# Side b of a two-sided attention layer: its queries three units ahead, its maxima two units ahead

## The chip, the cores and the metric

The kernel runs on one core of a Trainium2 chip. The metric is the device time of one execution in microseconds (us). TensorE (PE in the profile) multiplies matrices; its weight loads are listed as PEld. VectorE (DVE), ScalarE (ACT) and GpSimd (POOL) work on tiles, and SyncE (SP) issues every DMA of this kernel. Each engine takes its instructions from a queue of its own, in order.

## The reference

A decoder layer on 1024 tokens of width 1024, batch 1. After a modulated layer norm one wide projection gives the inputs of two attention branches and their gates:

```
qa = _rope(q_a...)                                    # side a: 2 groups of 4 heads, width 64
o_cmp, p_cmp = _compressed_attention(qa, kc, vc)      # over 63 compressed keys
sel_idx = _select_blocks(p_cmp, S)                    # 8 of 16 key blocks per query
o_sel = _selected_attention(qa, k_s, v_s, sel_idx)
o_win = _banded_attention(qa, k_w, v_w, 512)
qb = _rope(q_b...)                                    # side b: 2 groups of 4 heads
o_b = _banded_attention(qb, k_b, v_b, 128, sinks[l])  # softmax with one sink logit per head
merged = sigmoid(gm_a) * (y_a @ w_up_a) + sigmoid(gm_b) * (y_b @ w_up_b)
out = merged @ w_out;  x = layer_norm(ALPHA*x + gate*out) * ln_g + ln_b
```

Every score is divided by 8 (the square root of the head width) ahead of its softmax. All is float32; the kernel reaches it with pairs of narrower matmuls (a high part and the rest).

## The kernel before

**Stages.** First the layer norm, the modulation and the key and value projections; then one long attention stage (`Att.run`); then the outputs' transposes, the up projections, the output projection and the last norm.

**Units.** `Att.run` walks over 32 units (side, group, tile of 128 queries): (a,0,0) to (a,1,7), then (b,0,0) to (b,1,7). A unit has three parts.
- `C(u)` makes its queries. ACT copies q into the high half of `qat` (L752) and POOL takes the rest (L753); ACT copies q into `qbt` (L755); PE turns `qat` (L759) into a PSUM bank, and ACT copies that into `qa` (L761). On side a it also does the compressed attention and the block selection.
- `M(u)` finds each query's maximum. PE multiplies `qa` with the keys (`bank<-Ks,qa` and `bank<-Kw,qa` in the profile; side b has two banks of two matmuls per unit), DVE takes the masked maximum of each head (L878) and the negated result into `qbt` (L882); on side b POOL and ACT make the sink's term `esink` (L885, L886); PE turns `qbt` (L890) and ACT copies that into `qb` (L892). C and M share three PSUM banks, taken in turn.
- Per key tile, `score` multiplies the keys with `qa` and with `qb` into one bank, so that the maximum is already taken off. DVE adds a mask where one is needed (L907), ACT takes the exponential `e` (L909 or L911) and its f16 copy `ph` (L914), POOL the rest `pl` (L917); `weigh` then multiplies `pl` and `ph` with the values. A side b unit has two key tiles (one for tile 0). `combine` scales the result and SP stores it (`o_raw<-q`, L958).

**Order.** While unit i is weighed, M of unit i+1 and C of unit i+2 are made (`part` after each key tile, `finish` at the end). There are two `qbt` tiles and three `qa` tiles. Between these steps `feed` puts in "fill": projections that the attention does not need yet, in blocks (`gm_block`, four weight loads and 48 matmuls of 512 columns; side b's query projections; side b's keys). A fill weight comes by a DMA into one of three `raw` tiles (issued by SP at L245 or L257), ACT casts its high part into `whl` (L248, L259), POOL subtracts for the low part (L249, L260), and PE uses both with `uH` and `uL`. There are ten `whl` tiles. A scheduler then sets the order on each engine from its own model of time; what it made is fixed in the program.

The 1/8 is folded into the query's rotation tables: three ACT multiplications (L1173) make `qcos` and `qsin` from `cos`, `nsin` and `sin`. POOL copies or adds `sink` as it comes from memory (L1147).

Of the kernel before, what the change touches and what calls it, by code (L numbers as in the profile page):

```python
# [7 lines left out]
F32 = mybir.dt.float32  # L8
# [19 lines left out]
POFF = math.log(16.0)  # L28
XB = 8
# [686 lines left out]
class Att:  # L716


    def __init__(self, L, q, work):

        self.L, self.q, self.w = L, q, work
        self.ms, self.st, self.av = Banks(L, MS), Banks(L, ST), Banks(L, (5,))
        nc = L.nc
        self.nc = nc
        self.U = {}
        self.qbt = []
        for i in range(2):
            q = work.tile([128, 4, 128], F32R, name=f"qbt{i}")
            nc.gpsimd.tensor_copy(q.rearrange("p h d -> p (h d)"), L.mk[:, 128:129].to_broadcast([128, 512]))
            self.qbt.append(q)  # L730
        self.p0 = work.tile([128, 128], F32, name="p0")[:, :68]
        nc.gpsimd.memset(self.p0, 0.0)
        self.n, self.last = 0, []
        self.off = [True, True]
# [9 lines left out]
    def C(self, u):  # L744
# [6 lines left out]
        qbt = st["qbt"] = self.qbt[self.n % 2]  # L751
# [8 lines left out]
        qa = st["qa"] = w.tile([128, 512], F32R, name="qa", tag="qa", bufs=3)  # L760
        nc.scalar.copy(qa, tr.bitcast(F32).rearrange("p h t -> p (h t)"))  # L761
        yield 0.25
        if side == "b":
            self.rows_off(self.n % 2)
            return
# [4 lines left out]
        t = w.tile([128, 4, 64], F32, name="cs", tag="cs")  # L770
        nc.vector.tensor_tensor(t, sc[:, :, 1, :], L.vis[:, qt, None, :].to_broadcast([128, 4, 64]), op=OP.add)
        nc.vector.tensor_tensor(t, t, sc[:, :, 0, :], op=OP.add)
        sm = w.tile([128, 4, 8], F32, name="csm", tag="csm", bufs=2)[:, :, :4]
# [3 lines left out]
        nc.scalar.activation(e, t, AF.Exp)  # L777
# [4 lines left out]
        pc = w.tile([128, 4, 64], F32, name="cp", tag="cp")  # L782
# [6 lines left out]
        if qt >= 4:  # L789
            nc.vector.tensor_reduce(self.p0[:, 1:64], pc[:, :, 0:63].rearrange("p h c -> p c h"), axis=AX.X, op=OP.add)  # L790
            im = w.tile([128, 4, 16], F32, name="imp", tag="imp")
# [3 lines left out]
            m8 = w.tile([128, 40], F32, name="m8", tag="m8")[:, :8]  # L795
            nc.vector.max(m8, im[:, 1])
            nc.vector.match_replace(im[:, 2], m8, im[:, 1], -3e38)
            sel = st["sel"] = w.tile([128, 16], F32, name="sel", tag="sel", bufs=3)
# [9 lines left out]
        pT = w.tile([128, 2, 128], F32, name="pT", tag="pT")  # L808
# [20 lines left out]
    def M(self, u):  # L829
# [53 lines left out]
        if side == "b":  # L883
            es = st["es"] = w.tile([128, 2, 4], F32, name="esink", tag="esink", bufs=3)
            nc.gpsimd.tensor_tensor(es[:, 0], L.sink[:, g * 4:g * 4 + 4], qbt.bitcast(F32)[:, :, 80 + g], op=OP.add)  # L885
            nc.scalar.activation(es[:, 1], es[:, 0], AF.Exp, bias=L.poff)  # L886
# [9 lines left out]
    def score(self, u, br, kt):  # L896
# [9 lines left out]
        if kt == qt or edge:  # L906
            nc.vector.tensor_tensor(e.rearrange("p (h q) -> p h q", h=4), ps.rearrange("p (h q) -> p h q", h=4),  # L907
                                    L.mkt[:, int(edge), None, :].to_broadcast([128, 4, 128]), op=OP.add)
            nc.scalar.activation(e, e, AF.Exp, bias=L.poff)  # L909
        else:  # L910
            nc.scalar.activation(e, ps, AF.Exp, bias=L.poff)  # L911
# [48 lines left out]
    def run(self, units, fill, ratio, values):  # L960
# [52 lines left out]

        def part(f, u, k, n):
# [4 lines left out]
            while s[1] < want:  # L1019
                s[1] += 1  # L1020
                try:
                    feed(next(s[0]))
                except StopIteration:
                    s[1] = 1 << 30

# [15 lines left out]
        for gi, grp in enumerate(groups):  # L1041
# [24 lines left out]
            if k == n:  # L1066
                if ui + 1 < len(units):
                    finish(self.M, units[ui + 1])
                if ui + 2 < len(units):
# [54 lines left out]
def run_layer(L):  # L1124
# [22 lines left out]
    nc.sync.dma_start(L.sink, bass.AP(tensor=I["sinks"].tensor, offset=I["sinks"].offset, ap=[[0, 128], [1, 8]]))  # L1147
    acc = L.acc1
# [45 lines left out]
    def q_chunk(side, g, rows):  # L1194
# [3 lines left out]
        for t in ORD[side][g]:  # L1198
# [5 lines left out]
            L.rope(q, a[:, :256], t, qp, nc.vector, L.qcos, L.qsin)  # L1204
# [96 lines left out]
    for cm in (wk_cm, kvb[0], k0_cm, k1_cm, qp_cm):  # L1301
        L.close(cm)
# [214 lines left out]
```

## Time and profile before

| | |
|---|---|
| median of 3 runs | 943.93 us (943.79 to 946.45) |
| the profiled execution: its time, its span | 945.29 us, 943.5 us |
| PE busy, PEld busy | 914.3 us (97%), 787.0 us (83%) |
| POOL, DVE, ACT busy | 575.6, 550.2, 471.4 us |
| mean granted TensorE clock | 0.994 of full speed |

The span is the time from the first instruction to the last in the profile; the time around it holds 1.8 us more. The profiled execution was 1.4 us over the median. A busy engine is one that has an instruction under way; for PE this counts pipelined matmuls, so that small gaps between two matmuls do not show. Times in the trace are counted from the span's start.

### The profile page before, as it was taken

The numbers are of one execution on the slowest core, as the hardware profiler recorded it, in microseconds if no ns is written. First come the engines' busy times: TensorE is split into PE (matmuls) and PEld (weight loads), VectorE is DVE, ScalarE is ACT, GpSimd is POOL, SyncE is SP. The second block draws the span as 40 slices with busy tenths as digits, with TensorE's granted clock in tenths as the row PEclk, the third lists the DMA queues.
The fourth block names the chain that finished last, engine by engine and source line by source line (L and its number), as shares of the span: only waits on it lengthen the run. The fifth ranks groups of instructions, "written<-read, shape, count | busy, mean of one in ns | idle before, by whom it ended". The sixth has DMA issues, their size and how long they took to land.

```text
span 943.5 us, 18610 instructions
## 1 busy us (share of the span) xinstructions
PE 914.3 (97%) x6592; PEld 787.0 (83%) x6592; DVE 550.2 (58%) x1621; ACT 471.4 (50%) x984; POOL 575.6 (61%) x808
## 2 busy tenths in 40 slices
PE   7899998999999999999999999999899999999996
PEld 5689997788899888898899888789788888888885
DVE  7843356554776554465786643456552666454687
ACT  5846344344555566646555555756663664532100
POOL 7867565365768766767677766756753245535822
PEclk9999999999999999999999999999989999999999
DMA  9913232212202211202201212030222977655312
GB/s 329 293 29 115 81 91 57 79 51 79 68 7 53 62 57 57 63 13 70 76 7 35 74 58 75 22 101 13 69 62 75 371 249 221 192 188 193 130 69 110
DMA packets 93278, 95.40 MB, mean 101 GB/s; under 512 B 7616, under 2 KB 72192, under 8 KB 93184
## 3 DMA queue, kind: packets, MB, share of 16 engines
q1 hardware_dynamic: 93184, 94.21, 31.9%
q8 instruction: 52, 0.85, 0.4%
q14 instruction: 42, 0.34, 0.1%
HBM read 73.21 MB, written 20.97 MB: 100 GB/s over the span
## 4 chain that ended last, share of the span: by engine, by line
PE 69%; DMA 8%; DVE 8%; POOL 7%; ACT 3%; issue 3%; SPq 1%; DVEq 0%; POOLq 0%; ACTq 0%
PE bank L108 65%; DMA sg<-gm_raw 2%; POOL z L1421 2%; DMA raw<-in_w_ada_dram 2%; DMA raw<-in_w_out_dram 1%; DMA raw<-in_w_in_dram 1%; POOL rstd L1444 1%; DVE res L1450 1%; POOL pl L917 1%; PE bank L890 1%; DVE jk L878 1%; DMA x<-in_x_dram 1%; PE bank L759 1%; POOL whl L260 1%; PE bank L1327 1%
## 5 line engine op out<-in xcount | busy, mean ns | idle before, releaser
L108 PE MATMUL bank<-whl,uH 128*128 128x256 f32 (+3 forms) x1168 | 270.6, 322 | 4.6 <-ACT uH L449 4.3
L108 PE MATMUL bank<-uH,whl 128*128 128x512 f32 x768 | 247.5, 397 | 0.0
L917 POOL TENSOR_TENSOR pl<-e,ph 128x512 f16<-128x512 f32 x162 | 188.1, 1167 | 66.4 <-ACT ph L914 58.1
L108 PEld LDWEIGHTS bank<-whl,uH 128*128 128x128 f32 x1168 | 197.9, 189 | 22.2 <-ACT uH L449 5.3
L108 PE MATMUL bank<-whl,uL 128*128 128x256 f32 (+3 forms) x584 | 181.3, 319 | 0.0
L108 PEld LDWEIGHTS bank<-uH,whl 128*128 128x128 f32 x768 | 142.1, 189 | 26.8
L260 POOL TENSOR_TENSOR whl<-raw,whl 128x256 fp32r<-128x256 f32 x128 | 99.1, 779 | 86.6 <-ACT whl L259 78.6
L108 PE MATMUL bank<-uL,whl 128*128 128x512 f32 x384 | 151.3, 394 | 0.0
L108 PEld LDWEIGHTS bank<-whl,uL 128*128 128x128 f32 x584 | 110.1, 189 | 7.4
L914 ACT CAST ph<-e 128x512 f16<-128x512 f32 x162 | 98.4, 618 | 25.1 <-PE bank L108 23.1
L878 DVE CUSTOM_DVE_ANT_0 jk<-bank,mk 128x256 bf16<-128x256 f32 (+3 forms) x168 | 73.9, 440 | 30.0 <-PE bank L108 25.4
L911 ACT ACTIVATE e<-bank,poff 128x512 f32<-128x512 f32 x92 | 62.0, 687 | 54.0 <-PE bank L108 50.3
L108 PEld LDWEIGHTS bank<-uL,whl 128*128 128x128 f32 x384 | 72.6, 189 | 14.9
L259 ACT CAST whl<-raw 128x256 fp32r<-128x256 f32 x128 | 50.8, 404 | 66.0 <-PE bank L108 42.2
L108 PE MATMUL bank<-yH,whl 128*128 128x512 f32 x256 | 79.1, 393 | 0.0
L108 PEld LDWEIGHTS <-pl 128*128 128x128 f16 x648 | 59.4, 98 | 17.1 <-issue 11.2
L249 POOL TENSOR_TENSOR whl<-raw,whl 128x256 fp32r<-128x256 f32 (+3 forms) x60 | 53.3, 895 | 24.1 <-ACT whl L248 22.8
L907 DVE TENSOR_TENSOR e<-bank,mkt 128x512 f32<-128x512 f32 x70 | 47.5, 688 | 33.0 <-PE bank L108 27.9
L108 PEld LDWEIGHTS <-ph 128*128 128x128 f16 x1296 | 65.2, 97 | 0.8 <-issue 0.5
L909 ACT ACTIVATE e<-e,poff 128x512 f32<-128x512 f32 x70 | 49.8, 721 | 30.5 <-DVE e L907 30.2
L248 ACT CAST whl<-raw 128x256 fp32r<-128x256 f32 (+3 forms) x72 | 34.2, 480 | 60.9 <-DMA raw<-in_w_out_dram 36.8
L108 PEld LDWEIGHTS bank<-yH,whl 128*128 128x128 f32 x256 | 47.7, 188 | 10.1 <-issue 0.5
(292 smaller groups left out, 1730.0 us busy)
## 6 DMA issues: line engine op xcount, KB each, us to landing
raw<-in_w_in_dram SPq DMA_DIRECT2D x136, 128.0 KB, 2.2
gm_raw<-gmo SPq DMA_DIRECT2D x48, 256.0 KB, 2.0
wada<-in_w_ada_dram SPq DMA_DIRECT2D x16, 512.0 KB, 6.0
sg<-gm_raw SPq DMA_DIRECT2D x32, 256.0 KB, 3.2
x<-in_x_dram SPq DMA_DIRECT2D x8, 512.0 KB, 5.1
o_raw<-q SPq DMA_DIRECT2D x32, 128.0 KB, 1.9
o<-o_raw SPq DMA_DIRECT2D x8, 512.0 KB, 6.7
z<-gm_raw SPq DMA_DIRECT2D x16, 256.0 KB, 6.7
```

Source lines behind the costliest of these rows:

```text
L108: return self.nc.tensor.matmul(out, l, r, start=start, stop=stop, skip_group_check=True)
L248: self.cast = nc.scalar.copy(h, raw).ins
L249: low = eng.tensor_tensor(l, raw, h.bitcast(F32), op=OP.subtract).ins
L259: nc.scalar.copy(hl[:, 0], raw)
L260: eng.tensor_tensor(hl[:, 1], raw, hl.bitcast(F32)[:, 0], op=OP.subtract)
L878: nc.vector.tensor_tensor_reduce(o, src, m, 1.0, -3e38, OP.add, OP.max, mx[:, h, g if side == "b" else bi, slots[h]:slots[h] + 1])
L907: nc.vector.tensor_tensor(e.rearrange("p (h q) -> p h q", h=4), ps.rearrange("p (h q) -> p h q", h=4), L.mkt[:, int(edge), None, :].to_bro ...
L909: nc.scalar.activation(e, e, AF.Exp, bias=L.poff)
L911: nc.scalar.activation(e, ps, AF.Exp, bias=L.poff)
L914: nc.scalar.copy(ph, e)
L917: eng.tensor_tensor(pl, e, ph, op=OP.subtract)
L1421: nc.gpsimd.tensor_scalar(z[:, t, :], z[:, t, :], ALPHA, None, op0=OP.mult)
```

## The change

It has three parts, and the scheduler orders the whole anew.

1. For side b the three parts are taken further ahead. While unit i of side b is weighed, the new `jobs` asks for `finish(M, i+1)` (the last turn of `qbt`) and all of `C(i+3)` after the first key tile, and for the scores and maxima of `M(i+2)` (`all_but` stops ahead of the turn) after the last.
2. For that, side b gets a third `qbt` tile and a fourth `qa` tile. They lie in a pool that takes the place of side a's own tiles (the compressed attention's), which move into a pool of their own that is closed when side b's first C is made. POOL fills the new `qbt` once.
3. The 1/8 moves from the query's tables into the exponentials (`scale=SCALE`), so the three multiplications at L1173 go; `sink` is multiplied by 8 once on POOL.

```diff
+SCALE = 0.125
+EORD = (1,0,1)
...
+        self.wx, self.wx_cm = L.pool("sidea", 1, side="right")
...
-        qbt = st["qbt"] = self.qbt[self.n % 2]
+        if side == "a":
+            qbt = self.qbt[self.n % 2]
+        else:
+            if len(self.qbt) == 2:
+
+                L.close(self.wx_cm)
+                self.wx, self.wx_cm = L.pool("sideb", 1, side="right")
+                self.qbt.append(self.wx.tile([128, 4, 128], F32R, name="qbt2"))
+                nc.gpsimd.tensor_copy(self.qbt[2].rearrange("p h d -> p (h d)"), L.mk[:, 128:129].to_broadcast([128, 512]))
+                self.nb = 0
+            i = (1, 2, 0)[self.nb % 3]
+            if i < 2:
+                self.rows_off(i)
+            qbt = self.qbt[i]
+            st["n"] = self.nb
+            self.nb += 1
+        st["qbt"] = qbt
...
-        qa = st["qa"] = w.tile([128, 512], F32R, name="qa", tag="qa", bufs=3)
+        if side == "b" and st["n"] % 4 == 1:
+            qa = self.wx.tile([128, 512], F32R, name="qa3", tag="qa3")
+        else:
+            qa = w.tile([128, 512], F32R, name="qa", tag="qa", bufs=3)
...
-            nc.scalar.activation(es[:, 1], es[:, 0], AF.Exp, bias=L.poff)
+            nc.scalar.activation(es[:, 1], es[:, 0], AF.Exp, bias=L.poff, scale=SCALE)
...
-            nc.scalar.activation(e, ps, AF.Exp, bias=L.poff)
+            nc.scalar.activation(e, ps, AF.Exp, bias=L.poff, scale=SCALE)
...
+        def all_but(f, u):
+
+            s = get(f, u)
+            while s[1] < 3:
+                s[1] += 1
+                feed(next(s[0]))
...
+        def jobs(ui):
+
+            b = 2 * NT
+            if ui == b - 2:
+                return [(finish, self.C, b + 1, 0)]
+            if ui == b - 1:
+                return [(finish, self.M, b, -6), (finish, self.C, b + 2, -3), (all_but, self.M, b + 1, -1)]
+            if ui >= b:
+                e = EORD
+                return [(finish, self.M, ui + 1, e[0]), (all_but, self.M, ui + 2, e[1]), (finish, self.C, ui + 3, e[2])]
+            return []
...
-            if ui + 1 < len(units):
+            if ui < 2 * NT - 1:
                 part(self.M, units[ui + 1], k, n)
-            if ui + 2 < len(units):
                 part(self.C, units[ui + 2], k, n)
+            for f, g, x, w in jobs(ui):
+                if x < len(units) and k == (w if w > 0 else n + w):
+                    f(g, units[x])
...
+    nc.gpsimd.tensor_scalar(L.sink, L.sink, 1.0 / SCALE, None, op0=OP.mult)
...
-    L.qcos = qp.tile([128, 8, 32], F32, name="qcos")
-    qsin = qp.tile([128, 2, 8, 32], F32, name="qsin")
-    L.qsin = (qsin[:, 0], qsin[:, 1])
-    for o, x in ((L.qcos, L.cos), (L.qsin[0], L.nsin), (L.qsin[1], L.sin)):
-        nc.scalar.mul(o, x, 0.125)
```

Apart from the operations of part 3, every engine keeps its order up to the weighing of (a,1,6), where the first C of side b is made (at 567 us in the trace of before). From there on the order is new. Three places of it follow; line numbers of the changed kernel are larger (L759 is L778 there, L890 is L912, L108 is L110, L257 is L259, L958 is L980, L259 is L261, L761 is L784, L892 is L914, L909 is L931, L914 is L936).

**PE, around the queries of (b,1,4).** Before: the turn of `qat` of (b,1,4), the first matmuls of two scores, the maxima's scores of (b,1,4), the turn of `qbt` of (b,1,3), the turn of `qat` of (b,1,5).

```order
L108 MATMUL bank_10386<-uL,whl 128x512
L759 MATMUL bank_10472<-idr,qat 128x128 x4
L108 MATMUL bank_10459<-qa,Kw_934 128x512
L108 MATMUL bank_10502<-qa,Kw_934 128x512
L108 MATMUL bank_10518<-Kw_934,qa 128x256 x2
L890 MATMUL bank_10452<-idr,qbt_1882 128x128 x4
L759 MATMUL bank_10583<-idr,qat 128x128 x4
```

With the change, from the turn of `qat` of (b,1,4) to its maxima's first scores (the row of bank_10538; the row of bank_10417 is the second half of those of (b,1,3)):

```order
L778 MATMUL bank_10359<-idr,qat 128x128 x4
L110 MATMUL bank_10391<-qb,Kw_930 128x512
L110 MATMUL bank_10417<-Kw_930,qa 128x256 x2
L110 MATMUL bank_10462<-qb,Kw_930 128x512
L110 MATMUL bank_10538<-Kw_930,qa 128x256 x2
```

and a little further on, from the second half of the maxima's scores of (b,1,5) to the turn of its `qbt` (L912), with the turn of `qat` of (b,1,6) (L778) and its maxima's first scores (bank_10716):

```order
L110 MATMUL bank_10634<-Kw_930,qa_10497 128x256 x2
L110 MATMUL bank_10662<-qa,Kw_930 128x512
L110 MATMUL bank_10662<-qb,Kw_930 128x512
L778 MATMUL bank_10594<-idr,qat 128x128 x4
L110 MATMUL bank_11316<-uH,whl 128x512
L912 MATMUL bank_10672<-idr,qbt_8325 128x128 x4
L110 MATMUL bank_10716<-Kw_930,qa 128x256 x2
```

The turn of the next unit's `qat` no longer stands right behind these; the distance from a turn to the scores that use it grew from two matmuls to four at (b,1,4), and is two short pieces at (b,1,6).

**SP, the fill weights between the stores of side b.** Before: one load (the first of a block of four), the stores of (b,0,4) to (b,0,7), one load, the store of (b,1,0), two loads, the store of (b,1,1), five loads.

```order
L257 DMA raw_10938<-in_w_in_dram 128x2x128
L958 DMA o_raw_73<-q_7573 128x256
L958 DMA o_raw_73<-q_7661 128x256
L958 DMA o_raw_73<-q_7739 128x256
L958 DMA o_raw_73<-q_7823 128x256
L257 DMA raw_10943<-in_w_in_dram 128x2x128
L958 DMA o_raw_73<-q_9701 128x256
L257 DMA raw_10948<-in_w_in_dram 128x2x128
L257 DMA raw_10953<-in_w_in_dram 128x2x128
L958 DMA o_raw_73<-q_9798 128x256
L257 DMA raw_11152<-in_w_in_dram 128x2x128
L257 DMA raw_11157<-in_w_in_dram 128x2x128
```

With the change, the same block of four (now raw_10944 to raw_10959) and the first load of the next block stand ahead of the stores of (b,0,5) to (b,1,0); behind these come three loads, the store of (b,1,1), and raw_11296.

```order
L259 DMA raw_10954<-in_w_in_dram 128x2x128
L1306 DMA gm_raw_72<-gmo_9780 128x512
L259 DMA raw_10959<-in_w_in_dram 128x2x128
L259 DMA raw_11158<-in_w_in_dram 128x2x128
L980 DMA o_raw_73<-q_7660 128x256
L980 DMA o_raw_73<-q_7738 128x256
L980 DMA o_raw_73<-q_7822 128x256
L980 DMA o_raw_73<-q_9848 128x256
L259 DMA raw_11163<-in_w_in_dram 128x2x128
L259 DMA raw_11168<-in_w_in_dram 128x2x128
L980 DMA o_raw_73<-q_9947 128x256
L259 DMA raw_11296<-in_w_in_dram 128x2x128
```

Four loads moved from behind those stores to ahead of them. (Between the last two loads and the last store stands raw_11173, of the same form.)

**ACT, the casts ahead of the queries' copies.** Before, ahead of the copy `qa` of (b,1,4), which is qa_10477:

```order
L892 CAST qb_10313<-bank3_10308 128x512
L755 CAST qbt1_1884<-q_10078 128x4x64
L259 CAST whl_10950<-raw_10948 128x256
L259 CAST whl_10955<-raw_10953 128x256
L259 CAST whl_11154<-raw_11152 128x256
L259 CAST whl_11159<-raw_11157 128x256
L909 ACTIVATE e_10321<-e_10321,poff_124 128x512
L761 CAST qa_10477<-bank2_10472 128x512
```

With the change, ahead of the copies `qb` of (b,1,4), which is qb_10588, and `qa` of (b,1,6), which is qa_10599:

```order
L261 CAST whl_11170<-raw_11168 128x256
L261 CAST whl_11175<-raw_11173 128x256
L931 ACTIVATE e_10528<-e_10528,poff_124 128x512
L914 CAST qb_10588<-bank3_10583 128x512
L936 CAST ph_10531<-e_10528 128x512
L261 CAST whl_11298<-raw_11296 128x256
L774 CAST qbt1_1880<-q_10518 128x4x64
L931 ACTIVATE e_10576<-e_10576,poff_124 128x512
L784 CAST qa_10599<-bank4_10594 128x512
```

Four casts stood in a row ahead of a query's copy; now there are two and one, with other work between.

## Rows read from the trace of the kernel before

**Rows 1.** Busy time by stage: stretch (us), its length, then per engine busy us and count of instructions, the mean granted clock, the share of DMA, GB/s.

```profile
575.00:615.00 40.00, 39.30 (x356) 31.31 (x354) 15.36 (x54) 30.36 (x62) 29.37 (x41) 1.00 0.14 44
615.00:665.00 50.00, 48.51 (x468) 44.12 (x467) 29.73 (x114) 30.50 (x66) 31.04 (x54) 1.00 0.17 54
665.00:725.00 60.00, 56.98 (x452) 48.07 (x452) 27.96 (x100) 32.33 (x68) 33.83 (x51) 0.94 0.22 60
725.00:943.50 218.50, 210.37 (x979) 174.81 (x977) 136.87 (x201) 70.82 (x133) 95.94 (x75) 0.99 0.57 191
```

**Rows 2.** The same view in pieces of one us, in the third of these stretches.

```profile
680.00:681.00 1.00, 0.38 (x1) 0.06 (x1) 0.76 (x5) 0.63 (x2) 0.15 (x1) 1.00 0.63 141
681.00:682.00 1.00, 0.08 (x1) 0.08 (x1) 0.00 (x0) 1.00 (x3) 0.58 (x1) 1.00 0.47 125
...
683.00:684.00 1.00, 0.31 (x3) 0.34 (x3) 0.50 (x3) 1.00 (x3) 0.94 (x4) 0.66 0.29 86
684.00:685.00 1.00, 1.00 (x6) 0.90 (x5) 0.00 (x0) 1.00 (x4) 1.00 (x2) 0.50 0.00 0
...
690.00:691.00 1.00, 1.00 (x16) 0.73 (x15) 0.00 (x0) 0.00 (x0) 0.00 (x0) 0.92 0.19 74
```

**Rows 3.** PE in order of time there: start, us, engine, line, operation and tiles, forms, count, and in brackets the idle time ahead of it and what ended it.

```profile
676.26 0.62 PE L108 MATMUL bank<-uH,whl 128*128 128x512 f32 x2
676.72 0.40 PE L108 MATMUL bank<-uL,whl 128*128 128x512 f32 x1
...
679.02 0.46 PE L759 MATMUL bank<-idr,qat 128*128 128x128 f32 x4
...
681.92 0.50 PE L108 MATMUL bank<-Kw,qa 128*128 128x256 f32 x2 [1.55 <-ACT qa L761]
...
683.69 0.72 PE L759 MATMUL bank<-idr,qat 128*128 128x128 f32 x4 [0.97 <-DVE mx L878]
```

**Rows 4.** PE's other waits in side b, from the same view.

```profile
603.15 0.19 PE L108 MATMUL bank<-Vw,pl 128*128 128x65 f16 x1 [0.48 <-POOL pl L917]
...
637.38 0.54 PE L890 MATMUL bank<-idr,qbt 128*128 128x128 f32 x4 [0.27 <-DVE qbt L882]
...
638.75 0.20 PE L108 MATMUL bank<-Vs,pl 128*128 128x65 f16 x1 [0.53 <-POOL pl L917]
...
660.26 0.46 PE L759 MATMUL bank<-idr,qat 128*128 128x128 f32 x4
661.40 0.53 PE L890 MATMUL bank<-idr,qbt 128*128 128x128 f32 x4 [0.68 <-DVE qbt L882]
...
705.31 0.53 PE L890 MATMUL bank<-idr,qbt 128*128 128x128 f32 x4 [0.41 <-DVE qbt L882]
```

**Rows 5.** ACT in order of time ahead of the wait at 681.92.

```profile
676.87 0.79 ACT L259 CAST whl<-raw 128x256 fp32r<-128x256 f32 x2 [2.44 <-DMA raw<-in_w_in_dram]
...
680.37 0.40 ACT L259 CAST whl<-raw 128x256 fp32r<-128x256 f32 x1 [1.48 <-DMA raw<-in_w_in_dram]
680.68 0.72 ACT L909 ACTIVATE e<-e,poff 128x512 f32<-128x512 f32 x1
681.30 0.56 ACT L761 CAST qa<-bank 128x512 fp32r<-128x512 f32 x1
```

**Rows 6.** SP in order of time: the issues of DMAs; a row of several stands for the time from the first to the last.

```profile
643.72 23.52 SPq L958 DMA_DIRECT2D o_raw<-q  x4
670.98 0.38 SPq L257 DMA_DIRECT2D raw<-in_w_in_dram  x1
...
673.01 1.08 SPq L257 DMA_DIRECT2D raw<-in_w_in_dram  x2
...
675.84 6.14 SPq L257 DMA_DIRECT2D raw<-in_w_in_dram  x5
```

**Rows 7.** DVE in order of time: two maxima of one bank and the reduction into `qbt`.

```profile
680.19 0.42 DVE L878 CUSTOM_DVE_ANT_1 jk<-bank,mk 128x256 bf16<-128x256 f32 x1
...
680.66 0.18 DVE L882 TENSOR_REDUCE qbt<-mx 128x8 fp32r<-128x24 f32 x1
```

**Rows 8.** The page, part 6: the loads of the fill weights (count, KB each, median us from issue to landing).

```profile
raw<-in_w_in_dram SPq DMA_DIRECT2D x136, 128.0 KB, 2.2
```

**Rows 9.** The line of the copy after the turn of `qat`: count, duration in ns (least, median, most), first and last start.

```profile
L761 ACT CAST qa<-bank x32: 564/580/595, 146.4 to 705.2; 128x512 fp32r<-128x512 f32 x32
```

**Rows 10.** ACT by line and form: an exponential without a scale, and the multiplications that go, which are activations with a constant scale of 0.125.

```profile
L777 ACT ACTIVATE cs<-cs 128x256 f32<-128x256 f32 x16 | 6.6, 414 | 20.6 <-POOL cs L775 20.6
...
L1173 ACT ACTIVATE qcos<-cos 128x256 f32<-128x256 f32 x1 | 0.4, 413 | 0.0
```

**Rows 11.** The sink's load, POOL around 30 us, and POOL's fill of a `qbt` tile at the start of the stage.

```profile
L1147 SPq DMA_DIRECT2D sink<-in_sinks_dram x1: 3072/3072/3072, 23.2 to 23.2; - x1
...
DMA to landing us min/median/max: 6.3/6.3/6.3
...
24.73 0.22 POOL L536 TENSOR_SCALAR lnv<-lnv 128x1 f32<-128x1 f32 x1
...
28.93 1.25 POOL L249 TENSOR_TENSOR whl<-raw,whl 128x496 fp32r<-128x496 f32 x1 [0.73 <-ACT whl L248]
31.70 4.31 POOL L450 TENSOR_TENSOR uL<-lnT,uH 128x256 fp32r<-128x256 f32 x5 [1.53 <-ACT uH L449]
...
L729 POOL CAST qbt<-mk 128x512 fp32r<-128x512 f32 x2 | 1.2, 605 | 0.0
```

More of the change, by code (lines that the diff above doesn't have):

```diff
@@ L759, in C @@
             self.last.append(nc.tensor.transpose(tr[:, h, :], qat[:, h].rearrange("p a d -> p (a d)"), L.idr).ins)
-        qa = st["qa"] = w.tile([128, 512], F32R, name="qa", tag="qa", bufs=3)
+        if side == "b" and st["n"] % 4 == 1:
+            qa = self.wx.tile([128, 512], F32R, name="qa3", tag="qa3")
+        else:
+            qa = w.tile([128, 512], F32R, name="qa", tag="qa", bufs=3)
+        st["qa"] = qa
         nc.scalar.copy(qa, tr.bitcast(F32).rearrange("p h t -> p (h t)"))
@@ L763, in C @@
         if side == "b":
-            self.rows_off(self.n % 2)
             return
@@ L769, in C @@
                              L.kcd[:, g].rearrange("p i c -> p (i c)"), True, True).ins)
-        t = w.tile([128, 4, 64], F32, name="cs", tag="cs")
+        t = self.wx.tile([128, 4, 64], F32, name="cs", tag="cs")
         nc.vector.tensor_tensor(t, sc[:, :, 1, :], L.vis[:, qt, None, :].to_broadcast([128, 4, 64]), op=OP.add)
         nc.vector.tensor_tensor(t, t, sc[:, :, 0, :], op=OP.add)
-        sm = w.tile([128, 4, 8], F32, name="csm", tag="csm", bufs=2)[:, :, :4]
+        sm = self.wx.tile([128, 4, 8], F32, name="csm", tag="csm", bufs=2)[:, :, :4]
         nc.vector.tensor_reduce(sm[:, 0], t, axis=AX.X, op=OP.max)
@@ L776, in C @@
         e = t
-        nc.scalar.activation(e, t, AF.Exp)
+        nc.scalar.activation(e, t, AF.Exp, scale=SCALE)
         yield 0.45
@@ L781, in C @@
         nc.gpsimd.tensor_tensor(e, e, sm[:, 2, :, None].to_broadcast([128, 4, 64]), op=OP.mult)
-        pc = w.tile([128, 4, 64], F32, name="cp", tag="cp")
+        pc = self.wx.tile([128, 4, 64], F32, name="cp", tag="cp")
         nc.vector.scalar_tensor_tensor(pc.rearrange("p h c -> p (h c)"), e.rearrange("p h c -> p (h c)"), TINY,
@@ L790, in C @@
             nc.vector.tensor_reduce(self.p0[:, 1:64], pc[:, :, 0:63].rearrange("p h c -> p c h"), axis=AX.X, op=OP.add)
-            im = w.tile([128, 4, 16], F32, name="imp", tag="imp")
+            im = self.wx.tile([128, 4, 16], F32, name="imp", tag="imp")
             nc.vector.tensor_reduce(im[:, 0], self.p0[:, 0:64].rearrange("p (j i) -> p j i", i=4), axis=AX.X, op=OP.add)
@@ L794, in C @@
             nc.gpsimd.tensor_tensor(im[:, 1], im[:, 0], L.forced[:, qt], op=OP.add)
-            m8 = w.tile([128, 40], F32, name="m8", tag="m8")[:, :8]
+            m8 = self.wx.tile([128, 80], F32, name="m8", tag="m8")[:, :8]
             nc.vector.max(m8, im[:, 1])
             nc.vector.match_replace(im[:, 2], m8, im[:, 1], -3e38)
-            sel = st["sel"] = w.tile([128, 16], F32, name="sel", tag="sel", bufs=3)
+            sel = st["sel"] = self.wx.tile([128, 16], F32, name="sel", tag="sel", bufs=3)
             nc.vector.tensor_scalar(sel, im[:, 2], -2e38, NEG, op0=OP.is_gt, op1=OP.mult)
@@ L807, in C @@
             self.last.append(nc.tensor.transpose(tp[:, j, :], pc[:, 2 * j:2 * j + 2, :].rearrange("p h c -> p (h c)"), L.idf).ins)
-        pT = w.tile([128, 2, 128], F32, name="pT", tag="pT")
+        pT = self.wx.tile([128, 2, 128], F32, name="pT", tag="pT")
         nc.scalar.copy(pT, tp)
@@ L883, in M @@
         if side == "b":
-            es = st["es"] = w.tile([128, 2, 4], F32, name="esink", tag="esink", bufs=3)
+            es = st["es"] = w.tile([128, 2, 8], F32, name="esink", tag="esink", bufs=3)[:, :, :4]
             nc.gpsimd.tensor_tensor(es[:, 0], L.sink[:, g * 4:g * 4 + 4], qbt.bitcast(F32)[:, :, 80 + g], op=OP.add)
-            nc.scalar.activation(es[:, 1], es[:, 0], AF.Exp, bias=L.poff)
+            nc.scalar.activation(es[:, 1], es[:, 0], AF.Exp, bias=L.poff, scale=SCALE)
         yield 0
@@ L908, in score @@
                                     L.mkt[:, int(edge), None, :].to_broadcast([128, 4, 128]), op=OP.add)
-            nc.scalar.activation(e, e, AF.Exp, bias=L.poff)
+            nc.scalar.activation(e, e, AF.Exp, bias=L.poff, scale=SCALE)
         else:
-            nc.scalar.activation(e, ps, AF.Exp, bias=L.poff)
+            nc.scalar.activation(e, ps, AF.Exp, bias=L.poff, scale=SCALE)
         ph = w.tile([128, 512], F16, name="ph", tag="ph", bufs=PB)
@@ L1066, in run @@
             if k == n:
-                if ui + 1 < len(units):
+                if ui < 2 * NT - 1:
                     finish(self.M, units[ui + 1])
-                if ui + 2 < len(units):
                     finish(self.C, units[ui + 2])
@@ L1203, in q_chunk @@
             q = qp.tile([128, 256], F32, name="q", tag="q", bufs=QB)
-            L.rope(q, a[:, :256], t, qp, nc.vector, L.qcos, L.qsin)
+            L.rope(q, a[:, :256], t, qp, nc.vector)
             rows[side, g, t] = q
@@ L1300, in run_layer @@
     fill.rest()
-    for cm in (wk_cm, kvb[0], k0_cm, k1_cm, qp_cm):
+    for cm in (A.wx_cm, wk_cm, kvb[0], k0_cm, k1_cm, qp_cm):
         L.close(cm)
```

## The prediction

> **What bounds the kernel now.** I read the busy times first. TensorE is busy for 97% of the span, so only its idle time and its clock can give anything back. The change reorders side b, so I cut that part out by stage [rows 1]: from 575 to 725 us PE is idle for 0.70, 1.49 and 3.02 us, 5.2 us in all, and the third stretch alone has a granted clock under full, 0.94. Before 567 us the order stays, and the 8.1 us after 725 lie in stages without attention.
>
> [...] Six us at half the clock give three us of full-speed work, so about 3.1 us are lost there, with the edges. In order of time [rows 3], two waits lead to it: 1.55 us for the copy `qa` of (b,1,4), then 0.97 us for DVE's maxima, ahead of the turn of (b,1,5), which takes the bank that they read. The other waits are 0.48, 0.27, 0.53, 0.68 and 0.41 us [rows 4]: two for `pl`, three for the reduction that ends the maxima.
>
> Why was `qa` late? PE had turned the queries by 679.5, but ACT reached the copy at 681.30 [rows 5]: it stood in its queue behind an exponential and behind casts of fill weights that waited for their DMAs (2.44 us ahead of 676.87, 1.48 ahead of 680.37). And why were these late? On SP, which issues in order, their loads stood behind stores of finished units [rows 6]: four stores from 643.72 to 667.24, one load at 670.98, two at 673.01, five from 675.84. A load lands 2.2 us after its issue [rows 8], and with three `raw` tiles the loads of one burst wait for each other's casts. So the worst wait of side b is a weight load behind a store, passed on by ACT's queue.
>
> **The change part by part.** PE's matmuls are the same in number and size, so nothing is taken from its 97%; the terms are waits.
>
> *The loads.* By the new order on SP, the whole block of four and one load of the next stand ahead of the four stores, where one load stood before: four loads no longer wait for these units. On ACT four casts in a row stood ahead of `qa` of (b,1,4); now the casts there are one or two at a time, with exponentials and copies between them. Saved: 1.55 + 0.97 = 2.5 us.
>
> *The clock.* With that pair of waits gone, what PE did ahead of the fall is gone too. Saved: 3.1 us, or nothing if new waits lie as close together.
>
> [...]
>
> *The maxima.* From the last scores of a unit to the turn of its `qbt`, DVE needs two maxima at 0.47 us from start to start and 0.18 us for the reduction [rows 7], 1.1 us. At (b,1,1) the order left it one score matmul and one turn, 0.23 + 0.30 us (a matmul of 512 columns starts 0.23 us after the one ahead [rows 3]), so 0.6 us short: the trace shows 0.68 us of wait [rows 4]. With the change the turn comes in the next unit, behind a weighing and a score, and from (b,0,0) to (b,1,3) at least 1.8 us of PE work lie between, counted on the order with the spacing of such rows. The three waits of this kind (0.27, 0.68, 0.41) and the wait of 0.53 for `pl` at 638.75 go, the last because the new order has at least 4 us between a score and its weighing where before it had 3.2: saved 1.9 us. The 0.48 at 603.15 stays: there POOL is at its busiest (29.4 of 40 us [rows 1], with side a's `pl` still coming), and it gets 0.6 us more to do, the fill of the third `qbt` tile, by the same operation at the stage's start [rows 11].
>
> *New waits.* The copy after a turn takes 0.58 us [rows 9] (`qb` has the same size as `qa`), so about 0.65 from the turn to the matmul that uses them. Near the end of the units the new order is tight. At (b,1,4) the scores come four pieces after the turn, 0.7 us: enough. At (b,1,6) they come one fill matmul and one turn later, 0.53 us: 0.1 short. At (b,1,5) the turn of `qbt` comes 1.0 us after the scores: 0.15 short; at (b,1,4) likewise 0.1. The copy `qb` of (b,1,4) stands on ACT behind two casts and an exponential, and `qa` of (b,1,6) behind a cast and an exponential. ACT's starts are 0.31 us apart after a cast and 0.62 after an exponential [rows 5], which by my count makes each of the two copies 0.4 us late. That makes 1.2 us by distances and queues. The same reckoning of the two places shown of before gives 0.6 us at (b,1,1) and 0.2 at (b,1,4), 0.8 in all, where the trace has 0.68 + 1.55 = 2.2. So distances give the lower end, 1.2, and 2.8 times that the upper, 3.4. I take 2.5, nearer the upper end, since ACT's queue stays as crowded.
>
> *The scale.* No row shows an exponential with a scale, but the multiplications that go are activations with a constant scale: 413 ns against 414 for an exponential of the same size without one [rows 10]. So it costs nothing. Their going frees 1.2 us of ACT once, ahead of the attention; I count nothing for it.
>
> *The sink.* POOL's new multiplication stands ahead of the run of `uL` subtractions at 31.70. Its load is issued at 23.2 and lands 6.3 us later, at 29.5; POOL is free at 30.18 and idle until 31.70 [rows 11]. An operation on one column takes 0.22 us there. It costs nothing unless the load lands 2 us later than here, and from then on at most what it is late.
>
> *After side b.* Two weight loads of the last block now stand behind the loads of the outputs and gates, where all stood ahead. PE comes to them some 20 us after the last weighing; I count nothing.
>
> **The sum.** −2.5 − 3.1 − 1.9 + 2.5 = −5.0 us. Against the profiled execution's own 945.3 us that is 940.3; it was 1.4 us over the median of the runs, so against 943.93 it is 938.9, rounded to 939.0 us.
>
> **The rivals.**
> 1. *The waits regroup and the clock still falls.* For it: the tight places of the new order lie within some 10 us, around (b,1,3) to (b,1,6), as those of before did. Against it: none is next to another by more than 0.5 us by distance. Then 3.1 us are not saved: −1.9, 942.0 us.
> 2. *What is gained is given back after 725 us,* by the loads that moved behind the outputs', or because the queries' transposes were moved in the code but not by the scheduler (at (b,1,4) they still stand only 0.7 us ahead of their scores). For it: DMA is the fuller there, 0.57 of its time against 0.22 before [rows 1]. Against it: 20 us of slack. 943.9 us.
> 3. *Slower: the fill weights of the new burst.* Three loads now stand behind the store of (b,1,0), and raw_11296 behind that of (b,1,1), with 4.5 us of PE work from that unit's last weighing to its first use; two issues at 0.38, the landing at 2.2 and a cast at 0.40 make 3.4 of it [rows 5, 6, 8], and the unit's last scaling and the weight's subtraction come on top. If each of these five casts held PE for 1.55 us, as the one before did [rows 3], 7.75 us come in with the clock down as now, and 2.5 + 1.9 go: +3.4, 947.3 us. It decides from waits of 7.2 us on. Against it: of seven such casts before, one reached PE.
> 4. *Slower: the sink.* If its load landed at 39.5 in place of 29.5, POOL would hold `uL` and PE's first projections for 7.8 us, which with −5.0 is 946.7 us; less delay only eats into the gain. The load's 6.3 us to landing here speak against it.
>
> **How the numbers follow.** The likeliest, 939.0 us, gets 0.56 and runs from 935.6 (no new wait: 943.9 − 5.2 − 3.1) to 941.1, where 0.3%, about what a measurement of this kernel can tell from no change, begins. Rival 1 gets 0.20, rival 2 0.08, rival 3 0.10, rival 4 0.02; 0.04 is left for small changes of another kind, within the same bound. So: faster 0.56, same 0.32, slower 0.12. For 8 in 10 the range goes from 935.6 to 945.5, past rivals 1 and 2, and leaves out rivals 3 and 4 and the tails.
>
> **What would show it.** Right: no wait of over 1 us on PE between 580 and 725 us, a granted clock of 1.00 throughout, and side b shorter by 4 to 6 us with the stages around it unchanged. Waits for `qbt`'s reduction mostly gone, those for `qa` and `qb` near the last units of 0.2 to 0.8 us each. POOL's multiplication of the sink in the gap ahead of 31.70. Wrong: ACT waiting for a fill weight's DMA ahead of a query's copy again, or the clock at half anywhere in side b.

## The result, and the profile after

The changed kernel takes 938.94 us (median of 6 runs, 937.28 to 941.51), against 944.76 us for the kernel before (6 runs, 943.79 to 946.45): a ratio of 0.9939, 95% interval 0.9921 to 0.9956, or 5.8 us less. A second comparison (below), in which both kernels were slower, by 1.3 and 2.4 us, gave 0.9941. The profiled execution was the fastest of the six, 937.28 us with a span of 935.6, so the two traces differ by 8.0 us, more than the medians.

By stage, in the same columns as [rows 1]:

```profile
575.00:615.00 40.00, 39.89 (x375) 32.91 (x372) 15.74 (x61) 30.12 (x63) 29.35 (x41) 1.00 0.17 53
615.00:665.00 50.00, 50.00 (x428) 44.32 (x426) 25.71 (x89) 28.29 (x58) 28.59 (x48) 1.00 0.22 68
665.00:725.00 60.00, 57.53 (x504) 49.65 (x503) 33.29 (x119) 34.30 (x72) 35.78 (x55) 1.00 0.23 67
725.00:935.60 210.60, 202.81 (x946) 168.62 (x944) 136.15 (x197) 70.42 (x132) 94.90 (x74) 0.99 0.56 191
```

PE's idle time between 575 and 725 us fell from 5.21 to 2.58 us, and the third stretch has the full clock where it had 0.94. What is left stands in five waits of PE, in order of time (the start of a row is the end of its wait), of which the first is in the place of the 1.55 and 0.97 us of [rows 3]:

```profile
680.03 0.47 PE L110 MATMUL bank<-Kw,qa 128*128 128x256 f32 x2 [0.85 <-DVE mx L900]
...
686.81 0.47 PE L110 MATMUL bank<-qa,Kw 128*128 128x512 f32 x1 [0.61 <-DVE e L929]
...
688.60 0.51 PE L110 MATMUL bank<-qb,Kw 128*128 128x512 f32 x1 [0.29 <-ACT qb L914]
...
690.90 0.51 PE L912 MATMUL bank<-idr,qbt 128*128 128x128 f32 x4 [0.50 <-ACT qa L784]
...
692.32 0.50 PE L110 MATMUL bank<-Kw,qa 128*128 128x256 f32 x2 [0.21 <-ACT qb L914]
```

All of them lie in (b,1,3) to (b,1,6). ACT's waits for the DMA of a fill weight, 5.0 us in four waits between 575 and 725 before, are one of 0.3 (us in total, times, longest):

```profile
ACT whl L261 <- DMA raw<-in_w_in_dram: 0.3, 1, 0.3
```

The last store of side b is issued at 717.79 us, before at 725.59. Of these 7.8 us, 0.6 lie ahead of side b, where the order is the same (the turn of `qbt` of (a,1,6) starts at 539.68, before at 540.28; in the fourteen traces of this document it starts between 539.7 and 542.7, so this is spread). Behind side b nothing is gained or lost that counts (PE's last matmul starts at 927.53, before at 935.09).

### The profile page after: what moved, and what is told of

It is laid out like the page before. It is cut to its first block, busy times and chain, and to the rows that moved or that the text cites. A ratio compares the mean times of both kernels' runs of the same rounds, so it can differ in the third digit from the quotient of the medians.

```text
span 935.6 us, 18606 instructions
## 1 busy us (share of the span) xinstructions
PE 910.8 (97%) x6592; PEld 784.3 (84%) x6592; DVE 553.0 (59%) x1621; ACT 471.6 (50%) x981; POOL 576.1 (62%) x810
## 4 chain that ended last, share of the span: by engine, by line
PE 86%; DVE 5%; ACT 3%; POOL 2%; DMA 1%; issue 1%; SPq 0%; DVEq 0%; POOLq 0%; ACTq 0%
PE bank L110 82%; POOL rstd L1483 1%; DVE res L1489 1%; PE bank L912 1%; PE bank L778 1%; DMA x<-in_x_dram 1%; PE bank L1366 1%; DVE stats L1475 1%; DVE jk L900 1%; DVE z L1474 1%; DVE gt L1473 1%; DVE lnst L534 1%; ACT lnT L448 0%; DMA raw<-in_w_in_dram 0%; ACT lnT L474 0%
## 5 line engine op out<-in xcount | busy, mean ns | idle before, releaser
L110 PE MATMUL bank<-whl,uH 128*128 128x256 f32 (+3 forms) x1168 | 270.6, 322 | 3.2 <-ACT uH L451 2.8
L110 PE MATMUL bank<-uH,whl 128*128 128x512 f32 x768 | 245.9, 395 | 0.0
L110 PEld LDWEIGHTS bank<-whl,uH 128*128 128x128 f32 x1168 | 198.0, 189 | 21.0 <-ACT uH L451 3.9
L110 PE MATMUL bank<-whl,uL 128*128 128x256 f32 (+3 forms) x584 | 181.6, 319 | 0.0
L110 PEld LDWEIGHTS bank<-uH,whl 128*128 128x128 f32 x768 | 141.4, 188 | 26.8
L110 PE MATMUL bank<-uL,whl 128*128 128x512 f32 x384 | 150.5, 392 | 0.0
L110 PEld LDWEIGHTS bank<-whl,uL 128*128 128x128 f32 x584 | 110.1, 189 | 7.3
L936 ACT CAST ph<-e 128x512 f16<-128x512 f32 x162 | 98.7, 619 | 28.2 <-PE bank L110 26.3
L110 PEld LDWEIGHTS bank<-uL,whl 128*128 128x128 f32 x384 | 72.1, 188 | 14.9
L110 PE MATMUL bank<-yH,whl 128*128 128x512 f32 x256 | 79.1, 391 | 0.0
L261 ACT CAST whl<-raw 128x256 fp32r<-128x256 f32 x128 | 50.9, 404 | 51.4 <-PE bank L110 34.0
L110 PEld LDWEIGHTS <-pl 128*128 128x128 f16 x648 | 59.2, 98 | 15.6 <-issue 10.5
L110 PEld LDWEIGHTS <-ph 128*128 128x128 f16 x1296 | 64.7, 97 | 0.6 <-issue 0.3
L931 ACT ACTIVATE e<-e,poff 128x512 f32<-128x512 f32 x70 | 50.2, 723 | 29.3 <-DVE e L929 28.9
L110 PEld LDWEIGHTS bank<-yH,whl 128*128 128x128 f32 x256 | 48.0, 188 | 10.2 <-issue 0.5
```

The source lines that it names most:

```text
L110: return self.nc.tensor.matmul(out, l, r, start=start, stop=stop, skip_group_check=True)
L261: nc.scalar.copy(hl[:, 0], raw)
L931: nc.scalar.activation(e, e, AF.Exp, bias=L.poff, scale=SCALE)
L936: nc.scalar.copy(ph, e)
```

## The experiments

Ratios are to the kernel before, run beside the others, with 95% intervals. Its medians there were 945.9 to 946.5 us. The code shown is the lines that matter; "..." stands for the others.

**Which part of the change.** The scale alone, on the kernel before:

```diff
+            nc.scalar.activation(e, ps, AF.Exp, bias=L.poff, scale=SCALE)
-            nc.scalar.activation(e, ps, AF.Exp, bias=L.poff)
...
```

> The kernel before with part 3 alone: the 1/8 in the exponentials, the sink times 8 on POOL, the three multiplications gone. Every engine keeps the order of before in side b. Theory (the gain comes from the order of side b): as before, 943.5 to 945.5 us, with PE's waits of 1.55 and 0.97 us near (b,1,4) and the half clock behind them still there. Rival (the shorter ACT queue or the sink makes the gain): 938 to 941 us.

Measured 0.9991 (0.9981 to 1.0002), 945.3 us, with PE's waits of 1.5 and 0.9 us and half clock from 685 to 689: no part of the gain that can be told from none.

The look-ahead and its tiles without the scale:

```diff
-            nc.scalar.activation(e, ps, AF.Exp, bias=L.poff, scale=SCALE)
+            nc.scalar.activation(e, ps, AF.Exp, bias=L.poff)
...
```

> The changed kernel without part 3: the 1/8 back in the query's tables, look-ahead and buffers kept; the order of side b is that of the changed kernel. Theory: as the changed kernel, 937.5 to 940.5 us, no clock below full between 575 and 725 us. Rival (the scale is part of the gain): 941 to 944.

Measured 0.9957 (0.9942 to 0.9972), 941.97 us. In us this is the rival's range, but the kernel before was slower here too (946.51 us), and by the ratio it lies between the two ranges. The trace decides: the waits of side b are those of the changed kernel, of the same sizes, the clock is full from 575 to 725, and from the turn of `qbt` of (a,1,6) to the last weighing it takes 177.0 us, as the changed kernel does. The gain is in the order.

The changed kernel itself, a second time:

> The changed kernel once more, beside the kernel before on the chip of the runs below. Theory (order of side b, whatever the chip): a ratio to the kernel before of 0.993 to 0.996, and a clock that is full between 575 and 725 us. Rival (part of the 5.8 us was the chip's or the run's): a ratio of 0.996 to 0.999.

Measured 0.9941 (0.9918 to 0.9963), 941.34 us, and the clock full in side b.

The tiles without the look-ahead:

```diff
-            for f, g, x, w in jobs(ui):
-                if x < len(units) and k == (w if w > 0 else n + w):
-                    f(g, units[x])
...
-                if ui < 2 * NT - 1:
+                if ui + 1 < len(units):
                     finish(self.M, units[ui + 1])
```

> The changed kernel with the order of calls of before (queries two units ahead, maxima one), but with the third qbt tile, the fourth qa tile and the scale. Theory (the look-ahead makes the distance): 942 to 946 us, PE waits of 0.3 to 0.7 us for the reduction into qbt and at least one of over 1 us for a query's copy in (b,1,2) to (b,1,6). Rival (more tiles alone let the scheduler spread the work): 937 to 941.

Measured 1.0063 (1.0047 to 1.0078), 952.25 us: slower by 6 us, beyond both ranges. The clock falls three times in side b, in two of its stretches (their rows give PE's busy time, the granted clock, the share of DMA and GB/s), and near 677 us three waits follow each other:

```profile
575.00:615.00 40.00, 38.60 (x362) 0.96 0.14 43
...
665.00:725.00 60.00, 55.16 (x419) 0.94 0.19 54
```
```profile
675.48 0.47 PE L110 MATMUL bank<-Kw,qa 128*128 128x256 f32 x2 [0.40 <-DVE mx L900]
...
677.04 0.51 PE L778 MATMUL bank<-idr,qat 128*128 128x128 f32 x4 [0.79 <-DVE mx L900]
678.28 1.22 PE L110 MATMUL bank<-qb,Kw 128*128 128x512 f32 x2 [0.73 <-ACT qb L914]
```

The last row's two matmuls take 1.22 us, where the same pair took 0.63 at 672.80: the clock has fallen, at 678 us, within the third wait. None of the three waits reaches 1 us.

The look-ahead without the tiles:

```diff
-            i = (1, 2, 0)[self.nb % 3]
...
+            i = (1, 0)[self.nb % 2]
...
-        if side == "b" and st["n"] % 4 == 1:
-            qa = self.wx.tile([128, 512], F32R, name="qa3", tag="qa3")
...
```

> The changed kernel with the look-ahead, but two qbt tiles and three qa tiles as before. Theory (distance between the pieces, not tiles): 937 to 941 us, at most 1 us over the changed kernel. Rival (the look-ahead needs the tiles, since a copy into qbt or qa would wait for a turn or a score and hold ACT's queue): 942 to 946, with ACT waiting for a turn ahead of the copies into qbt or qa.

Measured 0.9953 (0.9937 to 0.9969), 941.68 us: between the two ranges in us, with the kernel before slower as well, and within the changed kernel's interval by the ratio. So the gain comes without the new tiles; whether they add a little cannot be told from these intervals.

**The cause that the prediction named: loads behind stores.**

```diff
+            elif n == 3:
+                for m in range(n, 2 * NT):
+                    nc.sync.dma_start(L.osp[2 + m // NT, :, m % NT, :], x)
```

> The kernel before, with the stores of the last twelve units of side b issued together at (b,0,3), of that unit's rows (the rows of the later units are left out of the result), so that no load on SP stands behind a store that waits; the other engines keep their order but for a few rows. Theory of the prediction (the loads are late behind the stores): PE's waits of 1.55 and 0.97 us near (b,1,4) and the half clock go, 938 to 941 us. Rival (the loads wait for POOL's subtractions, which free the three raw tiles, as SP's issues 0.02 us behind the ends of these suggest): waits and half clock as before, 944 to 947 us, at most 0.6 us less.

Measured 0.9994 (0.9982 to 1.0006), 945.78 us. No load stood behind a store that waits any more, and what it was to cure stayed: ACT waits 4.8 us for fill weights, and PE has the same two waits, with half clock from 684 to 688 behind them. Its PE, then SP and POOL of the same run:

```profile
682.54 0.51 PE L108 MATMUL bank<-Kw,qa 128*128 128x256 f32 x2 [1.59 <-ACT qa L761]
...
684.30 0.72 PE L759 MATMUL bank<-idr,qat 128*128 128x128 f32 x4 [0.96 <-DVE mx L878]
```
```profile
671.56 0.38 SPq L257 DMA_DIRECT2D raw<-in_w_in_dram  x1
...
673.58 0.37 SPq L257 DMA_DIRECT2D raw<-in_w_in_dram  x1
```
```profile
670.79 0.74 POOL L260 TENSOR_TENSOR whl<-raw,whl 128x256 fp32r<-128x256 f32 x1
...
672.81 1.44 POOL L260 TENSOR_TENSOR whl<-raw,whl 128x256 fp32r<-128x256 f32 x2
```

The first load leaves 0.03 us after the end of POOL's subtraction, and the second as the first of the pair ends: a load waits for the raw tile of three loads earlier. In the kernel before it was so too: POOL's row ends at 670.96, the first of its pair at 672.98, and SP's loads are at 670.98 and 673.01 [rows 6]. The third line is from SP's own waits there between 630 and 730 us (us in total, times, longest).

```profile
670.22 0.74 POOL L260 TENSOR_TENSOR whl<-raw,whl 128x256 fp32r<-128x256 f32 x1
...
672.25 1.43 POOL L260 TENSOR_TENSOR whl<-raw,whl 128x256 fp32r<-128x256 f32 x2
```
```profile
SPq L257 <- POOL whl L260: 14.6, 12, 3.7
```

Three weights, the last of them issued at 633.41 and landed at 636.03, lay in the three tiles until ACT's casts from 669.16 on, where its order had put them. Of the eight loads of that burst one, at 675.84, stood behind a store, for 0.6 us.

**One more raw tile**, on the kernel before with the scale, and on the changed one:

```diff
-        raw = rawp.tile([128, 2, n], F32, name="raw", tag="raw")
+        raw = xp.tile([128, 2, n], F32, name="rawx", tag="rawx") if xp else rawp.tile([128, 2, n], F32, name="raw", tag="raw")
...
+            w += L.load_w2(src[:, q * 2:q * 2 + 2, :], 128, rp, wp, nc.gpsimd, xp if q > 2 else None)
```

> The kernel before with the scale in the exponentials, and with a raw tile of its own for the fourth weight of each fill block (four loads can be under way in place of three); the scheduler orders the whole anew. Theory (three raw tiles pace the casts, the casts hold the queries' copies): ACT waits less than 1 us for fill weights' DMAs in side b, PE for no query's copy by more than 0.7 us, 939 to 942 us. Rival (the short distances of the maxima hold side b anyway): 943 to 947 us.

Measured 1.0035 (1.0020 to 1.0049), 948.97 us, slower than both ranges. Waits for `qa` fell to 0.4 at most, but the order is another one, and waits for the maxima stand elsewhere, next to each other as in the kernel with the tiles alone. Three of 0.40, 0.79 and 0.84 us, which end from 674.66 to 677.57, are followed by a fall of the clock at 679; this pair is not:

```profile
716.53 0.54 PE L891 MATMUL bank<-idr,qbt 128*128 128x128 f32 x4 [0.80 <-DVE qbt L883]
717.74 0.53 PE L109 MATMUL bank<-qb,Kw 128*128 128x512 f32 x1 [0.68 <-ACT qb L893]
```

> The changed kernel with a raw tile of its own for the fourth weight of each fill block. Theory (with the look-ahead PE no longer waits for what the loads hold up): as the changed kernel within 1.5 us, 938 to 942 us. Rival (loads still hold side b): 934 to 937 us.

Measured 0.9941 (0.9921 to 0.9961), 940.8 us, as the changed kernel. So the loads, whatever holds them, do not bound side b of the changed kernel.

**The theory of distances.** After these runs I counted on each kernel's order what the expectation below says, with the starts of PE's rows as prices (about 0.23 us per matmul of 512 columns). Each of its sums for the next four kernels was made before that kernel ran.

Maxima two ahead, queries two ahead:

```diff
-                return [(finish, self.M, ui + 1, e[0]), (all_but, self.M, ui + 2, e[1]), (finish, self.C, ui + 3, e[2])]
+                return [(finish, self.M, ui + 1, e[0]), (finish, self.C, ui + 2, e[2]), (all_but, self.M, ui + 2, e[1])]
```

> Side b's maxima two units ahead, its queries two units ahead as before (made just ahead of the scores that use them); tiles and scale of the changed kernel. The theory of distances, formed from the runs so far: a part is late where PE's order leaves less work than 0.65 us between the turn of the queries and their first scores, 1.3 between the last scores of the maxima and the turn of qbt, 0.65 between that turn and the score that uses it, 3.6 between a score and its weighing; counted on the orders, what is short in side b sums to 3.4 us for the kernel before, 0.95 for the changed one, 3.8 for the two kernels that were slower than before. Here it is 6.7 us, near (b,1,0) to (b,1,4) above all: 948 to 953 us, a ratio of 1.002 to 1.007, with half clock in side b. Rival (the maxima's look-ahead makes the gain): 0.993 to 0.997.

Measured 1.0051 (1.0032 to 1.0071), 951.72 us, as the theory had it. Three waits end within 3.6 us of each other; the clock is half from 674 to 681 and again from 698 to 701.

```profile
672.32 0.49 PE L110 MATMUL bank<-qa,Kw 128*128 128x512 f32 x1 [0.99 <-DVE e L929]
673.93 0.79 PE L110 MATMUL bank<-Kw,qa 128*128 128x256 f32 x2 [0.68 <-ACT qa L784]
675.87 0.79 PE L110 MATMUL bank<-qb,Kw 128*128 128x512 f32 x1 [0.68 <-ACT qb L914]
```

Queries three ahead, maxima one:

```diff
-                return [(finish, self.M, ui + 1, e[0]), (all_but, self.M, ui + 2, e[1]), (finish, self.C, ui + 3, e[2])]
+                return [(finish, self.C, ui + 3, e[2])]
...
+            if ui + 1 < len(units):
+                part(self.M, units[ui + 1], k, n)
```

> Side b's queries three units ahead, its maxima one unit ahead as before; tiles and scale of the changed kernel. By the theory of distances what is short sums to 0.2 us: a ratio to the kernel before of 0.990 to 0.995, PE's waits in side b under 2 us in all, no half clock there. Rival (the maxima's look-ahead makes the gain, the queries' does not): 0.998 to 1.006.

Measured 0.9960 (0.9944 to 0.9976), 942.92 us: most of the gain, but outside the theory's range and the rival's, and with 3.7 us of waits where under 2 were forecast. No wait for a maximum exceeds 0.3 us, but two long ones came that distances on PE cannot show: 1.83 us for `pl`, which stood on POOL behind a weight's subtraction, `qat` and the scaling of side a, with half a clock from 608 to 611; and 1.41 for `qa`, behind casts, exponentials and `ph` on ACT.

```profile
607.00 0.20 PE L110 MATMUL bank<-Vw,pl 128*128 128x65 f16 x1 [1.83 <-POOL pl L939]
...
687.27 0.50 PE L110 MATMUL bank<-Kw,qa 128*128 128x256 f32 x2 [1.41 <-ACT qa L784]
```

Another place for the three jobs, with less fill in side b, and then without that:

```diff
-EORD = (1,0,1)
+EORD = (1,1,0)
...
-RATIO = {'start': 9.0, 'e': 0.9, 'a': 1.25, 'b': 1.0}
+RATIO = {'start': 9.0, 'e': 0.9, 'a': 1.25, 'b': 0.9}
```

> The changed kernel with the queries of three units ahead made after the last key tile and the scores of the maxima after the first (EORD 1,1,0 in place of 1,0,1), and 0.9 in place of 1.0 for the share of fill in side b. By the theory of distances nothing is short in side b: PE's waits there under 1.5 us in all, no half clock, a ratio to the kernel before of 0.989 to 0.993, 1.5 to 3 us better than the changed kernel. Rival (the waits left in the changed kernel have another cause and come back, or the fill that moves out of side b costs elsewhere): 0.993 to 0.997.

Measured 0.9906 (0.9886 to 0.9926), 937.72 us: 0.9% faster than the kernel before, and the best of all runs (its interval just overlaps those of the changed kernel, whose ratios are 0.9939 and 0.9941). Its side b is 2.5 us shorter than the changed kernel's (174.5 against 177.0 us from the turn of `qbt` of (a,1,6) to the last weighing). PE is idle for 0.15 us from 575 to 725, with the full clock:

```profile
575.00:615.00 40.00, 39.88 (x372) 32.65 (x369) 15.11 (x59) 29.59 (x61) 28.97 (x41) 1.00 0.14 44
615.00:665.00 50.00, 50.00 (x490) 45.89 (x489) 32.40 (x120) 31.41 (x65) 33.19 (x55) 1.00 0.19 57
665.00:725.00 60.00, 59.97 (x468) 50.27 (x467) 28.28 (x96) 32.22 (x70) 34.23 (x52) 1.00 0.30 88
```

> The changed kernel with EORD 1,1,0 alone, the share of fill in side b left at 1.0. By the theory of distances 0.26 us is short: a ratio to the kernel before of 0.990 to 0.994, PE's waits in side b under 2 us in all, no half clock there. Rival (the share of fill of 0.9 made the gain of the last run): 0.993 to 0.997, as the changed kernel.

Measured 0.9947 (0.9932 to 0.9961), 940.62 us, as the changed kernel. PE's waits there are 1.3 us as the theory said (0.64 for `qbt`, 0.39 for a mask's sum, 0.29 for a weight), yet the time is the rival's. Its trace has a fall of the clock at 190 us, in side a, that the trace of the kernel ahead lacks, but that is not the difference: at the turn of `qbt` of (a,1,6) both stand alike, at 541.55 and 541.58 us. From there to the last weighing this one takes 179.6 us and the one with the share of 0.9 takes 174.5; it has 1.5 us more of waits there, and 539 matmuls on fill weights against 530, by an estimate at 0.23 us each about 2 us. What lies behind that takes 1.0 us less in this one. So with this place of the jobs the step to 0.9906 needs the smaller share of fill; what that share does with the jobs in their old place was not run.

Of the theory's four sums, two gave the time (1.0051 and 0.9906) and two did not (0.9960 and 0.9947).

## Why the prediction was right, and where its reasons were not

**The time** was right: 939.0 forecast, 938.94 measured, 5.8 us less against 5.0. That the two times meet to 0.1 us is luck: the median of the kernel before rose from 943.93 to 944.76 us with three more runs, and the terms below miss in both directions.

**"The loads", −2.5 us: the wait went, the cause was wrong.** The 1.55 and 0.97 us are gone, replaced by one of 0.85 at 680.03. But the step that put the lateness on stores ahead of the loads on SP failed. The loads waited for POOL's subtractions, which free the three raw tiles (14.6 us in twelve waits of SP, above), and freeing SP of the stores changed nothing. I had seen stores and loads in one queue in [rows 6] and taken order for cause; SP's list of releasers was the view to read. One step further the cause fails as well: with a fourth raw tile the wait for `qa` shrinks, and the time grows. What the look-ahead changed is the distance on PE between a part and its user, and with it how close the waits lie; that this is what shortens side b is argued from the orders, by a theory that gave two of four times.

**"The clock", −3.1 us: right that it goes, and the larger lesson; the size was that of one trace.** The half clock in side b is gone in all five traces with the look-ahead of the changed kernel and its order of jobs (the two of it, and those without the scale, without the tiles, with the fourth raw tile). The three traces with the order of before have it, at the same place behind the same two waits. In the trace that the prediction read it is at 0.50 from 684 to 690; there the starts of four matmuls of 512 columns take 1.70 us (687.31 to 689.01), 0.43 us each in place of 0.23. But it lasts 6.8 us there and 3.4 us in the two others, which by the granted clock of 0.50 makes an estimated 1.7 us. These have a granted clock of 0.97 in the third stretch in place of 0.94 (the kernel with early stores, then the one with the scale alone):

```profile
665.00:725.00 60.00, 56.95 (x460) 48.25 (x459) 28.96 (x102) 32.32 (x68) 34.39 (x51) 0.97 0.20 52
665.00:725.00 60.00, 57.14 (x469) 48.64 (x467) 28.42 (x101) 33.69 (x72) 35.46 (x55) 0.97 0.22 60
```

That the fall hangs on the waits alone was my supposition from one trace. What the fourteen traces show is that each of the ten falls in side b comes with waits. Eight come with two or three neighbours of 0.4 us and more (0.40, 0.79 and 0.73 us within 3 us, above), two with one longer wait, of 1.03 and of 1.83 us, and some under 0.2 beside it. The changed kernel's five waits from 680 to 693 us brought none, nor did the 1.41 us above. What tells the two apart no run here shows: the pair of 0.80 and 0.68 us at 717 us in the kernel before with the fourth raw tile brought no fall, and the same pair in the kernel with the tiles alone is followed by one at 719.

**"The maxima", −1.9 us: right and a little small.** The four waits are gone, and so is the 0.48 at 603.15 which was to stay: 2.4 us in place of 1.9.

**"New waits", +2.5 us: right in size, half right in place.** The five waits sum to 2.46 us. `qb` of (b,1,4) (0.29 at 688.60) and `qa` of (b,1,6) (0.50 at 690.90) were named, though at 690.90 it is not the scores that wait for the copy but the turn of `qbt` of (b,1,5), for the bank that the copy reads; the largest, 0.85, is a bank whose maxima DVE had not finished, and 0.61 is for a mask's sum on DVE, neither of which I had counted.

**The size.** By its own terms the sum is −2.5 − 3.1 − 2.4 + 2.5 = −5.5 us. From the turn of `qbt` of (a,1,6) to the last weighing of side b the trace of before takes 184.1 us (540.28 to 724.37) and that of the changed kernel 177.0 (539.68 to 716.63), 7.1 less and over the 4 to 6 us that were to show it right. The two other traces with the order of before take 182.4 and 182.7 us, the changed kernel's second trace 177.0 as well: against those two the gain is 5.5 to 5.7 us, near the 5.8 of the medians. The idle column that I summed counts from the modelled end of the matmul ahead. By an estimate from the starts of PE's matmuls (against the median spacing of the same two forms), some 13 us were lost from 567 to 735 us before and some 6.5 after, the clock included. Small gaps of some 0.15 to 0.36 us near 606, 680 and 706, which no bracket shows, are part of the rest; so is a wait of 0.19 at 606.46, which the prediction left out.

**At nothing: right as far as can be told.** The scale is worth 0.9 us by the middle of its interval, which holds zero, and side b takes as long without it. The sink's multiplication runs on POOL at 30.02, in the gap ahead of `uL`:

```profile
30.02 0.25 POOL L1191 TENSOR_SCALAR sink<-sink 128x8 f32<-128x8 f32 x1
31.47 4.32 POOL L452 TENSOR_TENSOR uL<-lnT,uH 128x256 fp32r<-128x256 f32 x5 [1.20 <-ACT uH L451]
```

**The rivals.** None came true for this change, but the first, regrouped waits with the clock down, is what three of the neighbouring kernels did (1.0035, 1.0051, 1.0063). Its 0.20 was not too much. The third, slower by weights behind stores, rested on the step that failed.

## What to carry to other kernels

Before a transfer is blamed on what stands ahead of it in its queue, read what released it: 0.03 us between the end of a buffer's last reader and the issue names the suspect, and a run without the stores settles it. Read a term of the clock from more than one trace of the same order. Where PE is 97% busy, count for each part the work that the order leaves between its making and its use (a count that missed two of four times here). Waits of 0.4 us and more near each other came with eight of the ten falls in side b here, and then both were paid, the waits and the half clock (1.55 and 0.97 us, and 6.8 us at half, in the trace that the prediction read). And try neighbouring orders: of eight others for this stage three were slower than the kernel before, and one had almost no wait left.

## What the runs showed that I had not expected

The same waits come with a fall of the clock in one execution and without one in another. The changed kernel's two traces have the same wait of 1.35 us for the first turn of `qat`, which ends at 143.39 and 144.47 us. In the first the clock stays up behind it, in the second it falls for 3.4 us (PE busy, granted clock, share of DMA, GB/s):

```profile
145.00:149.00 4.00, 3.83 (x33) 1.00 0.00 0
```
```profile
145.00:149.00 4.00, 4.00 (x22) 0.57 0.00 0
```

Nine of the fourteen traces have this wait of 1.35 us, and three of them the fall. Of the 4.0 us by which the second trace of the changed kernel is the longer, 1.1 were there at the wait already; by the turn of `qbt` of (a,0,0) it is 2.1 us behind, still 2.2 at the last weighing of side b, and the rest comes in behind side b. So the fall explains some 1.0 us of the 4.0. Three waits of 0.3, 0.4 and 0.6 us between 186 and 192 us, alike in every trace, come with a fall that starts at 190 to 192 in seven of fourteen. One trace of each kernel does not settle a difference of 2 us.
